# A hybrid decoder trunk: one PSUM tile for each of seven products, and 16 instead of 13 of 22 FFN double units by seven products

## The chip, the cores and the metric

The kernel runs on one core of one Trainium2 chip. Its time is the device time in microseconds of one execution; three runs are shown, and one more was taken with the hardware profiler.

## What is computed

The trunk has two layers of width 1024 over 512 tokens. The first layer mixes with stick-breaking and sparse attention heads, the second with forgetting attention; both layers end with the FFN that this change touches, and a final RMSNorm closes the kernel.

```python
def conv_glu_ffn(h, w_in, conv_w, conv_b, w_out):
    a, b = jnp.split(h @ w_in, 2, axis=-1)
    taps = conv_w[:, None, :]
    a = lax.conv_general_dilated(a, taps, window_strides=(1,), padding=[(CONV_WIDTH - 1, 0)], ...) + conv_b
    return (jax.nn.silu(a) * b) @ w_out

for layer in range(DEPTH):
    x = x + mixer(rmsnorm(x, attn_norm[layer]))
    x = x + conv_glu_ffn(rmsnorm(x, ffn_norm[layer]), ...)
return rmsnorm(x, final_norm)
```

D_FF is 2816, so each of `a` and `b` has 22 column blocks of 128.

## The kernel before, in words

Everything is kept transposed: features on the 128 partitions, the 512 tokens along the free dimension. Each fp32 operand of a matmul is split into a high and a low part (ScalarE casts the high part, VectorE subtracts it to get the low part), and each product of a block is three matmuls: high by high, low by high, high by low.

`ffn` (line 1073) runs once per layer. Its input projection is worked off in 22 **double units** (column block c of `a` and of `b`), its output projection in eight rows of `out` steps (`out`, line 1318) for each of four parts of the double units (`PARTS`, line 1070: units 0 to 5, 6 to 11, 12 to 16, 17 to 21). There are two kinds of double unit:

- `plain` (line 1157): two units of 8 contraction blocks, 24 matmuls of 512 columns each, into a PSUM tile `mm`; VectorE scales each result with `rstd` into `a` and `b`. The first `PLAIN` (line 1071) double units are of this kind.
- `seven` (line 1218): the four half-by-half blocks of tokens and contraction, for `a` and `b`, are formed from seven products of sums instead of eight products. Each product is 12 matmuls of 256 columns. The token sums (tiles `b1`, `b2`, `t1`, `t3`) are made once per FFN by `sums` (line 1191), on VectorE and GpSimd, during the plain units. The weight sums are made for every double unit: three on VectorE and one on GpSimd (`total`, line 1232, tile `sr`), each followed by a high and low split into one of eight slots (`part`, line 1241, tiles `sxh` and `sxl`). The slots are the buffers of the plain units' input, which the last plain unit frees step by step. The products (`product`, line 1265) come in the order a1, p2, p1, p4, p3, a2, b2, numbered 0 to 6. Product 3 uses part p4, whose sum needs the sums p1 and p2 first.

The readers of the seven products are one copy on ScalarE (product 0) and six additions or subtractions on VectorE, each of which also needs the one before it or two before it. After them `gate` and `gated` (lines 1104, 1121) apply the convolution, the activation and the product with `b`, and split the result into `gh` and `gl`, of which ten exist of each.

PSUM has eight banks, each 512 fp32 values wide: `mm` has two, `s` two tiles of two banks each, `t` and `o` one each. Before, products 0 and 1 shared one `s` tile, a bank for each; products 2 and 3 shared the next one; product 4 went to `o`, 5 to `t`, and 6 to a third `s` tile.

A planner (`Plan`, line 99) decides the order of all instructions of an FFN ahead of time. It takes each job's cost, the buffers it takes and gives, and a priority; on each engine the job of the best priority among those that can start goes next, and the order it finds is the program order of every engine. On TensorE a double unit (priority 100 + c) goes ahead of any out step (200 + part). All weight loads hang on SyncE's queue in one chain in program order (`M.prev_load`, lines 1229, 1230 and 1332): each waits until the one before it was issued, and for a free buffer. A second rule follows the tiles: a reader of a tile waits for the writers of that tile which stand before it in program order, and a writer for its earlier readers. Out steps of a part need the gated results of its double units, in their order.

The program order of the loads is set by the loops at the end of `ffn`:

```python
            for c in range(PLAIN):
                plain(c, root)
            ...
            done = PLAIN
            for p in range(1, len(PARTS)):
                c0, c1 = PARTS[p - 1]
                sevens(range(done, c1))
                done = max(done, c1)
                for m in range(NK):
                    if m % 2 == 0 and done < min(PARTS[p][1], c1 + 4):
                        seven(done)
                        done += 1
                    out(m, p - 1)
            sevens(range(done, NF))
```

With `PLAIN` = 9 that is: plain 0 to 8; seven 9; the eight out rows of part 0; sevens 10, 11, 12; two out rows of part 1; seven 13; two out rows; and so on to seven 21 and the out rows of part 3.

Below, a product 0 that starts at 440.54 us belongs to unit 10 of the first FFN, at 451.12 to unit 11, at 466.35 to unit 12. All instructions of the FFN are recorded by one helper, so the profile names line 83 for all of them; the tiles tell them apart.

Of the kernel before, what the change touches and what calls it, by code (L numbers as in the profile page):

```python
# [9 lines left out]
F32 = mybir.dt.float32  # L10
# [7 lines left out]
P = 128  # L18
SEQ = 512
# [15 lines left out]
class Fill:  # L35
# [5 lines left out]
    def add(self, *gens):  # L41
        self.q.extend([g, False] for g in gens)
# [115 lines left out]
def trunk(ctx, tc, A):  # L158
    nc = tc.nc
    inorder = [False]  # L160
    pe, act, dve, pool, sp = [Ordered(tc, e, inorder, e is nc.sync)
                              for e in (nc.tensor, nc.scalar, nc.vector, nc.gpsimd, nc.sync)]
# [4 lines left out]
    pp = EP(tc.tile_pool(name="pp", bufs=2, space=PSUM))  # L167

    def mm(out, l, r, st, sp_):
        pe.matmul(out, l, r, start=st, stop=sp_)  # L170

    def s_banks():
        return pp.tile([P, 2, SEQ], F32, tag="s", bufs=2, name="s")

    def s_bank():
        return s_banks()[:, 0]
# [891 lines left out]


    PARTS = ((0, 6), (6, 12), (12, 17), (17, 22))  # L1070
    PLAIN = 9

    def ffn(layer, nl, final):

# [4 lines left out]
        W = SEQ // 2  # L1079
        LO, HI = slice(0, W), slice(W, SEQ)  # L1080
        with ExitStack() as es:
# [3 lines left out]
                        a=2, tt=1, b=2, g=10, sr=2, slot=NK, sq=2)  # L1085
            plan.bufs["w"], plan.bufs["slot"] = [], []
            add = plan.add
# [6 lines left out]
            TJ = []  # L1094
# [62 lines left out]
            def plain(c, root):  # L1157
                box = {}
                ps = []
                for u in range(2):  # L1160
                    w = M.weights(A["wfi"][layer, 2 * c + u], [P, NK, P]) if c else (dict(h=first[u][0], l=first[u][1]), None)
                    lastu = (c, u) == (PLAIN - 1, 1)
                    bx, j = {}, None
# [51 lines left out]
            order = [None] * 3  # L1215
            count = [0]

            def seven(c):

                w, box, sm, sj = [None] * 4, {}, {}, {}  # L1220
                n0 = c * 0.001

                def load(u, pool_, tag):
                    def fn():
                        t = pool_.tile([P, NK, P], F32, tag=tag, bufs=2, name=tag)
                        sp.dma_start(t, A["wfi"][layer, 2 * c + u])
                        w[2 * u], w[2 * u + 1] = t[:, 0:H], t[:, H:NK]
                    return fn
                lb = add("SP", 0.35, load(1, fp, "wb"), M.prev_load, prio=1 + n0, take=("wb",), lat=3.3)
                la = M.prev_load = add("SP", 0.35, load(0, wp, "wraw"), lb, prio=1 + n0, take=("wraw",), lat=3.3)  # L1230

                def total(n, x, y, eng, *deps, give=()):
                    e = (pool, dve)[eng == "DVE"]

                    def fn():
                        sm[n] = wp.tile([P, H, P], F32, tag="sq", bufs=2, name="sr")
                        e.tensor_add(sm[n], x(), y())
                    sj[n] = order[2] = add(eng, 1.35 if eng == "POOL" else 0.69, fn, *deps, order[2], prio=1.2 + n0, take=("sr",), give=give)
                parts, pj = {}, {}

                def part(n, x, *deps, give=()):
                    def hi():
                        i = count[0] % NK
                        count[0] += 1
                        parts[n] = [xp.tile([P, H, P], F32R, tag=f"{t}{i}", name=f"s{t}") for t in ("xh", "xl")]
                        act.copy(parts[n][0], x())
                    j = order[0] = add("ACT", 0.62, hi, *deps, order[0], prio=1.2 + n0, take=("slot",))
                    pj[n] = add("DVE", 0.69, lambda: dve.tensor_sub(parts[n][1], x(), parts[n][0].bitcast(F32)), j, prio=1.2 + n0, give=give)
                E1, E3 = "DVE", "POOL"
                total("p1", lambda: w[2], lambda: w[3], E1, lb)  # L1250
                part("a1", lambda: w[0], la)
                total("p2", lambda: sm["p1"], lambda: w[0], "DVE", sj["p1"], la)
                part("p2", lambda: sm["p2"], sj["p2"])
                part("p1", lambda: sm["p1"], sj["p2"], give=("sr",))
                total("p4", lambda: sm["p2"], lambda: w[1], "DVE", pj["p2"], pj["p1"], give=("sr",))
                part("p4", lambda: sm["p4"], sj["p4"], give=("sr",))
                total("p3", lambda: w[0], lambda: w[2], E3, sj["p4"])
                part("p3", lambda: sm["p3"], sj["p3"], give=("sr",))
                part("a2", lambda: w[1], sj["p3"], give=("wraw",))
                part("b2", lambda: w[3], sj["p3"], give=("wb",))  # L1260

                s = []
                ev = []

                def product(j, n, m, take):
                    t, cols = MV[m]

                    def fn():
                        if take == "s":
                            s.append(s_banks())  # L1270
                        elif take:
                            s.append(pp.tile([P, 1, SEQ], F32, tag=take, bufs=1, name=take))
                        r = box[j] = s[-1][:, j % 2 if j < 4 else 0, 0:W]
                        h, l = parts[n]
                        for k in range(H):
                            xh, xl = B[t][0][:, k, cols], B[t][1][:, k, cols]
                            mm(r, h[:, k], xh, k == 0, False)
                            mm(r, l[:, k], xh, False, False)
                            mm(r, h[:, k], xl, False, k == H - 1)
                    order[1] = add("PE", 1.45, fn, pj[n], order[1], *TJ, prio=100 + c, take=(take,) if take else (), give=("slot",))  # L1280
                    return order[1]

                def take(eng, cost, fn, *deps, **k):
                    return add(eng, cost, fn, *deps, prio=1 + n0, **k)
                av = lambda h: box["a"][:, h]
                bv = lambda h: box["b"][:, h]

                def first_a():
                    box["a"] = fp.tile([P, SEQ], F32, tag="a", bufs=2, name="a")
                    act.copy(av(LO), box[0])  # L1290

                def first_b():
                    box["b"] = fp.tile([P, SEQ], F32, tag="b", bufs=2, name="b")
                    dve.tensor_sub(bv(LO), box[1], av(LO))

                def both():
                    b = box["b"].rearrange("p (h s) -> p h s", h=2)
                    dve.tensor_sub(b, b, box[4].unsqueeze(1).to_broadcast([P, 2, W]))
                j = product(0, "a1", "b11", "s")
                cp_ = take("ACT", 0.36, first_a, j, take=("a",))  # L1300
                j = product(1, "p2", "t2", None)
                u = take("DVE", 0.42, first_b, j, cp_, take=("b",), give=("s",))
                j = product(2, "p1", "t1", "s")
                v = take("DVE", 0.42, lambda: dve.tensor_sub(bv(HI), bv(LO), box[2]), j, u)
                j = product(3, "p4", "b22", None)
                c12 = take("DVE", 0.42, lambda: dve.tensor_sub(av(HI), box[3], bv(HI)), j, v, give=("s",))
                j = product(4, "p3", "t3", "o")
                c22 = take("DVE", 0.69, both, j, c12, give=("o",))
                j = product(5, "a2", "b21", "t")
                c11 = take("DVE", 0.42, lambda: dve.tensor_add(av(LO), av(LO), box[5]), j, u, give=("t",))  # L1310
                t = gate(c, box, c11, c12)
                j = product(6, "b2", "t4", "s")
                c21 = take("DVE", 0.42, lambda: dve.tensor_sub(bv(LO), bv(LO), box[6]), j, c22, give=("s",))
                gated(c, box, t, c21)
# [36 lines left out]
            def sevens(cs):  # L1351
                for c in cs:
                    seven(c)
            root = []
            for c in range(PLAIN):
                plain(c, root)
                if c == 0:
                    for k in range(H):
                        sums(k, root)
# [10 lines that stand above are left out]
# [265 lines left out]
```

## Time and profile before

| | |
|---|---|
| three runs | 1269.92, 1272.94, 1275.87 us; median 1272.94 |
| profiled execution | 1272.76 us, of which the span of instructions is 1271.0 us |
| granted TensorE clock, mean | 0.995 |
| busy: TensorE, VectorE, ScalarE, GpSimd | 98%, 70%, 49%, 17% of the span |
| HBM traffic | 119.28 MB read, 96 GB/s over the span |
| first FFN | about 299 to 655 us |
| second FFN | about 901 us to the end |

A row of the timeline has the start of an instruction from the start of the span, its duration, its engine, and the tile that it writes and those that it reads; in brackets stands how long the engine was idle before it and what ended that. PE is TensorE's matmuls, PEld its weight loads, DVE VectorE, ACT ScalarE, POOL GpSimd, SP SyncE. Matmuls are pipelined, so the next one starts well before the recorded end of the one before it; the pace of a stream is read from start to start.

### The profile page before, as it was taken

The page shows a single profiled execution, that of the slowest core. Times are in us where ns is not written, and L with a number is a line of the kernel's source. Part 1 is how long each engine was busy: PE and PEld are TensorE (multiplying, and loading weights), DVE is VectorE, ACT ScalarE, POOL GpSimd, SP SyncE. Part 2 cuts the span into 40 slices and gives each one's busy share as a digit, 9 for nine tenths or more (in the row PEclk, how much of TensorE's full clock was granted, in tenths as well). Part 3 has the DMA queues.
Part 4 walks back from the last instruction along what each step waited for, and adds up shares of the span by engine and source line. Part 5 has one row for each costly group of instructions (what it writes and reads, how often), then busy time and mean ns, then how long its engine had stood idle before and what let it go on. Part 6 is the DMA issues. An engine that isn't in the chain of part 4 may idle for free.

```text
span 1271.0 us, 18993 instructions
## 1 busy us (share of the span) xinstructions
PE 1243.6 (98%) x7268; PEld 1026.6 (81%) x7268; DVE 888.8 (70%) x1528; ACT 620.3 (49%) x1112; POOL 219.9 (17%) x266
## 2 busy tenths in 40 slices
PE   8999999999999999999999999999999999999997
PEld 5877776567888889999987777777788888999886
DVE  6776667548977489888863542534897759988874
ACT  5775446735543244444453654543554424444452
POOL 0000114303510000000030543300341000000011
PEclk9999999999999999999999999999999999999999
DMA  6313141112232333314233533312223233331321
GB/s 210 100 51 94 64 142 52 34 34 76 91 101 99 116 104 107 110 45 150 82 111 112 185 115 113 125 50 83 84 83 110 90 116 104 117 121 54 132 73 67
DMA packets 51418, 124.14 MB, mean 98 GB/s; under 512 B 6064, under 2 KB 17584, under 8 KB 51328
## 3 DMA queue, kind: packets, MB, share of 16 engines
q1 hardware_dynamic: 49808, 121.35, 29.7%
q10 hardware_dynamic: 1520, 1.59, 0.4%
q8 instruction: 57, 0.93, 0.3%
q14 instruction: 33, 0.27, 0.1%
HBM read 119.28 MB, written 2.13 MB: 96 GB/s over the span
## 4 chain that ended last, share of the span: by engine, by line
PE 89%; DVE 6%; ACT 3%; issue 1%; DMA 1%; SPq 0%; POOL 0%; DVEq 0%; POOLq 0%; ACTq 0%
PE mm L83 56%; PE s L83 20%; PE o L83 7%; PE t L83 7%; DVE xl L83 1%; DVE x L83 1%; DVE sxl L83 1%; DVE wlo L83 1%; ACT whi L83 0%; ACT sxh L83 0%; ACT e L83 0%; DMA x<-x 0%; DVE sr L83 0%; DVE acc L83 0%; ACT xh L83 0%
## 5 line engine op out<-in xcount | busy, mean ns | idle before, releaser
L83 PE MATMUL mm<-xh,whi 128*128 128x512 f32 x520 | 209.5, 403 | 1.6 <-ACT xh L83 1.0
L83 PE MATMUL mm<-xl,whi 128*128 128x512 f32 x520 | 203.7, 392 | 1.2 <-DVE xl L83 1.1
L83 PE MATMUL mm<-xh,wlo 128*128 128x512 f32 x520 | 203.2, 391 | 1.1 <-DVE wlo L83 1.1
L83 DVE TENSOR_TENSOR wlo<-wraw,whi 128x1024 fp32r<-128x1024 f32 (+3 forms) x95 | 114.8, 1208 | 47.0 <-ACT whi L83 46.6
L83 ACT CAST whi<-wraw 128x1024 fp32r<-128x1024 f32 (+3 forms) x95 | 96.5, 1016 | 90.3 <-PE mm L83 81.1
L83 PE MATMUL mm<-gh,wlo 128*128 128x512 f32 x332 | 129.9, 391 | 0.0
L83 PE MATMUL mm<-gh,whi 128*128 128x512 f32 x332 | 129.8, 391 | 0.0
L83 PE MATMUL mm<-gl,whi 128*128 128x512 f32 x332 | 129.2, 389 | 0.0
L83 DVE TENSOR_TENSOR x<-x,mm 128x512 f32<-128x512 f32 (+2 forms) x104 | 70.1, 675 | 77.0 <-PE mm L83 76.8
L83 PEld LDWEIGHTS mm<-xh,whi 128*128 128x128 f32 x520 | 97.7, 188 | 29.5 <-issue 7.9
L83 POOL TENSOR_TENSOR sr<-wraw,wb 128x512 f32<-128x512 f32 x26 | 36.6, 1408 | 485.2 <-DVE sr L83 359.5
L83 PEld LDWEIGHTS mm<-xl,whi 128*128 128x128 f32 x520 | 97.6, 188 | 24.5 <-DVE xl L83 3.7
L83 PEld LDWEIGHTS mm<-xh,wlo 128*128 128x128 f32 x520 | 97.8, 188 | 21.0 <-DVE wlo L83 2.1
L83 ACT CAST sxh<-sr 128x512 fp32r<-128x512 f32 x104 | 62.4, 619 | 76.9 <-DVE sr L83 59.4
L83 POOL TENSOR_SCALAR e<-e,dn 128x128 f32<-128x128 f32 (+3 forms) x128 | 70.3, 570 | 165.0 <-DVE dn L83 108.4
L83 ACT COPY ph<-t 128x512 f32<-128x512 f32 x100 | 58.5, 585 | 64.9 <-PE t L83 64.0
L83 ACT ACTIVATE e<-e,nm 128x128 f32<-128x128 f32 (+3 forms) x128 | 70.9, 557 | 31.6 <-DVE nm L83 31.6
L83 ACT ACTIVATE tt<-a,conv 128x512 f32<-128x512 f32 x44 | 36.0, 817 | 90.6 <-DVE a L83 90.3
L83 DVE TENSOR_TENSOR sxl<-sr,sxh 128x512 fp32r<-128x512 f32 x104 | 73.0, 724 | 9.3 <-ACT sxh L83 8.5
L83 DVE SCALAR_TENSOR_TENSOR tt<-a,conv,tt 128x510 f32<-128x510 f32 x88 | 72.9, 828 | 8.7 <-ACT tt L83 7.5
L83 ACT CAST whi<-wo 128x768 fp32r<-128x768 f32 (+1 forms) x60 | 47.0, 786 | 53.9 <-PE mm L83 47.9
L83 PEld LDWEIGHTS mm<-gl,whi 128*128 128x128 f32 x332 | 62.3, 188 | 13.2
(249 smaller groups left out, 3165.9 us busy)
## 6 DMA issues: line engine op xcount, KB each, us to landing
wraw<-wfi SPq DMA_DIRECT2D x62, 512.0 KB
wraw<-wu SPq DMA_DIRECT2D x31, 512.0 KB
wb<-wfi SPq DMA_DIRECT2D x26, 512.0 KB
wo<-wfo SPq DMA_DIRECT2D x32, 384.0 KB
wo<-wfo SPq DMA_DIRECT2D x28, 320.0 KB
wraw<-wo SPq DMA_DIRECT2D x16, 512.0 KB
wraw<-wv SPq DMA_DIRECT2D x10, 512.0 KB
cb<-cd SPq DMA_DIRECT2D x8, 512.0 KB
```

The source lines that it names most:

```text
L83: r = f(*a, **k)
```

## The change

The seven products each get a one-bank tile: 0, 2, 4 and 6 take `s` in turn, 1 and 5 take `t`, 3 takes `o`. The reader of each product gives its tile back. `s_bank` is the first bank of an `s` tile, so the second bank of these tiles stays unused here. `PLAIN` goes from 9 to 6, so that units 6, 7 and 8 of each FFN become sevens.

```diff
-    PLAIN = 9
+    PLAIN = 6
...
-                s = []
-                ev = []
-
                 def product(j, n, m, take):
                     t, cols = MV[m]
 
                     def fn():
                         if take == "s":
-                            s.append(s_banks())
-                        elif take:
-                            s.append(pp.tile([P, 1, SEQ], F32, tag=take, bufs=1, name=take))
-                        r = box[j] = s[-1][:, j % 2 if j < 4 else 0, 0:W]
+                            r = box[j] = s_bank()[:, 0:W]
+                        else:
+                            r = box[j] = pp.tile([P, SEQ], F32, tag=take, bufs=1, name=take)[:, 0:W]
...
-                    order[1] = add("PE", 1.45, fn, pj[n], order[1], *TJ, prio=100 + c, take=(take,) if take else (), give=("slot",))
+                    order[1] = add("PE", 1.45, fn, pj[n], order[1], *TJ, prio=100 + c, take=(take,), give=("slot",))
...
                 j = product(0, "a1", "b11", "s")
-                cp_ = take("ACT", 0.36, first_a, j, take=("a",))
-                j = product(1, "p2", "t2", None)
-                u = take("DVE", 0.42, first_b, j, cp_, take=("b",), give=("s",))
+                cp_ = take("ACT", 0.36, first_a, j, take=("a",), give=("s",))
+                j = product(1, "p2", "t2", "t")
+                u = take("DVE", 0.42, first_b, j, cp_, take=("b",), give=("t",))
                 j = product(2, "p1", "t1", "s")
-                v = take("DVE", 0.42, lambda: dve.tensor_sub(bv(HI), bv(LO), box[2]), j, u)
-                j = product(3, "p4", "b22", None)
-                c12 = take("DVE", 0.42, lambda: dve.tensor_sub(av(HI), box[3], bv(HI)), j, v, give=("s",))
-                j = product(4, "p3", "t3", "o")
-                c22 = take("DVE", 0.69, both, j, c12, give=("o",))
+                v = take("DVE", 0.42, lambda: dve.tensor_sub(bv(HI), bv(LO), box[2]), j, u, give=("s",))
+                j = product(3, "p4", "b22", "o")
+                c12 = take("DVE", 0.42, lambda: dve.tensor_sub(av(HI), box[3], bv(HI)), j, v, give=("o",))
+                j = product(4, "p3", "t3", "s")
+                c22 = take("DVE", 0.69, both, j, c12, give=("s",))
                 j = product(5, "a2", "b21", "t")
                 c11 = take("DVE", 0.42, lambda: dve.tensor_add(av(LO), av(LO), box[5]), j, u, give=("t",))
```

With `PLAIN` = 6 the loops above give: plain 0 to 5; seven 6, two out rows of part 0, seven 7, two out rows, seven 8, two out rows, seven 9, two out rows; sevens 10, 11, 12; and from there on as before.

## Rows read from the trace of the kernel before

**Rows 1.** The page, part 1: engine, busy us (share of the span), instructions

```profile
PE 1243.6 (98%) x7268; PEld 1026.6 (81%) x7268; DVE 888.8 (70%) x1528; ACT 620.3 (49%) x1112; POOL 219.9 (17%) x266
```

**Rows 2.** Three stretches, first FFN: busy us by engine, clock, DMA share, GB/s

```profile
366.00:440.00 74.00, 74.00 (x367) 62.98 (x367) 45.76 (x65) 25.59 (x37) 1.89 (x1) 1.00 0.33 108
...
440.00:492.00 52.00, 50.08 (x361) 47.27 (x360) 45.16 (x77) 24.40 (x43) 5.15 (x4) 0.97 0.27 92
...
492.00:560.00 68.00, 67.92 (x473) 63.32 (x472) 60.88 (x101) 31.47 (x54) 5.69 (x4) 1.00 0.32 100
```

**Rows 3.** Timeline of PE, second FFN: start us, us, engine, operation, out<-in

```profile
996.16 0.39 PE L83 MATMUL mm<-xh,whi 128*128 128x512 f32 x1
...
1001.60 0.28 PE L83 MATMUL s<-b1h,sxh 128*128 128x256 f32 x1
...
1090.91 0.28 PE L83 MATMUL o<-t3h,sxh 128*128 128x256 f32 x1
...
1092.35 0.28 PE L83 MATMUL t<-b2h,sxh 128*128 128x256 f32 x1
```

**Rows 4.** Timeline of PE: product 3 of units 10, 11 and their neighbours, both FFNs

```profile
444.85 0.28 PE L83 MATMUL s<-b2h,sxh 128*128 128x256 f32 x1
...
446.71 0.28 PE L83 MATMUL o<-t3h,sxh 128*128 128x256 f32 x1
...
457.13 0.38 PE L83 MATMUL s<-b2h,sxh 128*128 128x256 f32 x1 [0.15 <-ACT sxh L83]
459.13 0.58 PE L83 MATMUL s<-b2h,sxl 128*128 128x256 f32 x1 [1.61 <-DVE sxl L83]
...
459.72 0.41 PE L83 MATMUL s<-b2h,sxh 128*128 128x256 f32 x1
...
461.64 0.41 PE L83 MATMUL o<-t3h,sxh 128*128 128x256 f32 x1
...
1059.59 0.38 PE L83 MATMUL s<-b2h,sxh 128*128 128x256 f32 x1 [0.15 <-ACT sxh L83]
...
1062.99 0.28 PE L83 MATMUL o<-t3h,sxh 128*128 128x256 f32 x1
```

**Rows 5.** Timelines of PE and ACT: products 0 and 1 of units 10 and 12

```profile
443.29 0.28 PE L83 MATMUL s<-t1l,sxh 128*128 128x256 f32 x1
...
443.61 0.37 ACT L83 COPY a<-s 128x256 f32<-128x256 f32 x1 [3.12 <-PE s L83]
443.88 1.14 ACT L83 CAST sxh<-sr 128x512 fp32r<-128x512 f32 x2
...
467.67 0.28 PE L83 MATMUL s<-b1l,sxh 128*128 128x256 f32 x1
...
467.99 0.37 ACT L83 COPY a<-s 128x256 f32<-128x256 f32 x1 [1.03 <-PE s L83]
```

**Rows 6.** The tile sr, and one reader of the products: ns min/median/max

```profile
L83 DVE TENSOR_TENSOR sxl<-sr,sxh x104: 676/684/1381, 397.2 to 1219.7; 128x512 fp32r<-128x512 f32 x104
L83 DVE TENSOR_TENSOR sr<-sr,wraw x52: 679/686/693, 391.6 to 1216.1; 128x512 f32<-128x512 f32 x52
L83 POOL TENSOR_TENSOR sr<-wraw,wb x26: 1271/1296/1892, 401.6 to 1217.0; 128x512 f32<-128x512 f32 x26
...
L83 DVE TENSOR_TENSOR b<-b,s x52: 406/415/422, 403.9 to 1227.6; 128x256 f32<-128x256 f32 x52
```

**Rows 7.** Timelines of DVE and PE where the token sums end, first FFN

```profile
360.89 0.69 DVE L83 TENSOR_TENSOR t3l<-gl,t3h 128x512 fp32r<-128x512 f32 x1
...
361.06 0.39 PE L83 MATMUL mm<-xh,whi 128*128 128x512 f32 x1
```

**Rows 8.** Timeline of SP's queue, first FFN, like loads merged

```profile
385.73 42.23 SPq L83 DMA_DIRECT2D wo<-wfo  x8
```

**Rows 9.** Groups by line: busy us, mean ns, idle before; plain units on DVE

```profile
L83 DVE TENSOR_TENSOR wlo<-wraw,whi 128x1024 fp32r<-128x1024 f32 (+3 forms) x95 | 114.8, 1208 | 47.0 <-ACT whi L83 46.6
...
L83 DVE TENSOR_TENSOR a<-mm,rstd 128x512 f32<-128x512 f32 x18 | 12.4, 688 | 12.2 <-PE mm L83 12.1
```

## Prediction

> **What bounds the kernel now.** I read the page's busy table first: TensorE has work for 1243.6 of 1271.0 us [rows 1]. So only two things shorten the run: fewer matmul columns, or fewer holes in the matmul stream. Then I read the busy time by stretches of the first FFN [rows 2]: from 366 to 440 us and from 492 to 560 us TensorE is never or hardly idle (74.00 of 74, 67.92 of 68), but from 440 to 492 it lacks 1.92 us and its granted clock reads 0.97. VectorE is second: 0.62 of its time in the first of these stretches, 0.87 in the second, 0.895 in the third. Third comes the timeline of TensorE, for the pace of each kind of unit, for the places where the pace breaks, and for who is named there.
>
> **Fewer columns.** A plain double unit is two units of 24 matmuls; the last plain unit of the second FFN runs from 996.16 to 1001.60, so 5.44 us, and a double unit 10.88 us [rows 3]. A product of 12 matmuls goes from 1090.91 to 1092.35, 1.44 us; seven are 10.08 us [rows 3]. Exchanging one for the other saves 0.80 us. Three more in each of two FFNs: 6 x 0.80 = **4.8 us**, all on the path, since TensorE has no slack. The out steps, attention and the final stage are the same instructions.
>
> **The private PSUM tiles.** Products 0 and 1 lie in two banks of one tile, and so do 2 and 3. When product 1 follows product 0 at once, ScalarE's copy of product 0 should start when product 0's last matmul ends. In unit 10 it starts at 443.61, just behind the end of product 1's last matmul (443.29 + 0.28 = 443.57) [rows 5], and product 0 ended one product, 1.44 us, before that. In unit 12 an out step stands between the two, and the copy starts at 467.99, 0.04 us behind product 0's last matmul (467.67 + 0.28) while TensorE writes another tile [rows 5]. So the reader waits for the tile, 1.44 us too long, not for its bank. I count the adjacent case in six of the 13 units of each FFN. Queued behind the waiting copy on ScalarE is the cast of the fourth part (443.88 [rows 5]); behind that, VectorE's low half of this part; and product 3 waits for it.
>
> What it costs: in unit 10 product 3 takes 446.71 - 444.85 = 1.86 us in place of 1.44. In unit 11 it takes 461.64 - 457.13 = 4.51 us: VectorE's low half ends a wait at 459.13, and then matmuls come every (461.64 - 459.72) / 9 = 0.213 us in place of 0.12, the lower clock level (1.2 in place of 2.4 GHz) after that hole. The same unit of the second FFN takes 1062.99 - 1059.59 = 3.40 us, at full clock [rows 4]. Adding all smaller breaks in units whose product 1 follows at once, I get 4.84 us in the first FFN and 3.34 us in the second, 8.2 us in all; the three named here make 0.42 + 3.07 + 1.96 = 5.45 of it, and the largest others are the twin of unit 10's in the second FFN, the 0.3 us ahead of each of the two long products, and 0.3 us in unit 17 of each FFN. Units whose product 1 comes later lose only some 0.5 us together. With seven tiles the copy of 0 and the subtractions of 2 run one product earlier. Bounds on what comes back: 0 (the low half is late for want of VectorE time alone) to 8.2 us. I take **7.0**, nearer to the upper end, because the three stalls I can trace have a held copy ahead of them.
>
> The cost of the new tiles: product 1 now takes `t`, which product 5 of the unit before held; product 3 takes `o`; 4 takes `s`. At least two products (2.9 us) lie between a write and the next into the same buffer, and a subtraction takes 0.41 to 0.69 us [rows 6, 9]. I put this at nothing; the cover is those two products, and a reader later than that costs its excess.
>
> **The earlier start of the sevens.** Two orders change. First, the loads: SyncE's queue is a chain in program order. Before, the eight out-weight loads of part 0 (385.73 to 427.96 [rows 8]) stand ahead of unit 10's loads, so for 30 us TensorE does out steps only and VectorE idles, and then units 10 and 11 come with no out step left to fill their gaps. With six plain units the loads go 6, out, out, 7, out, out, 8, ..., 9, out, out, 10, 11, 12: the out steps, in front of which sevens always go, lie ready while VectorE catches up. That helps units 10 and 11 whatever the tiles do. Second, the sums of the tokens: their last VectorE step ends at 360.89 + 0.69 = 361.6, and plain unit 5's last unit, whose steps free the slots, begins at 361.06 [rows 7]. Before, 33 us lay between the sums and the first product; now none lie between the sums and the first parts, and 5.4 us to the first product (366.5). VectorE drops two weight splits of plain unit 6 (2 x 1.21 [rows 9]) and gains two sums of unit 6 (2 x 0.69 [rows 6]) there, so I do not see it later than now. Cost of this crossing: 0, to the 4 us of a start like that of units 10 and 11, per FFN. With the few tenths of a us that sevens lose elsewhere I take **1.5 us** for both FFNs.
>
> VectorE's load: a seven has 7 x 0.684 (low halves) + 3 x 0.686 (sums) [rows 6] + 5 x 0.415 + 0.69 (readers) = 9.6 us where a plain double unit has 2 x 1.21 + 2 x 0.69 = 3.8 [rows 9]: 5.8 more, 17.5 us in each FFN. From 366 to 560 it was busy 45.76 + 45.16 + 60.88 = 151.8 of 194 us [rows 2]; with 17.5 more in some 189 us that is 0.896, what the stretch from 492 to 560 already carries with 0.08 us of TensorE idle. It fits if the new order spreads it, with little to spare.
>
> One thing speaks against: GpSimd takes one of each seven's four sums (median 1.296 us), and beside it low halves last up to 1.381 in place of 0.684 us [rows 6]; six of 182 do. The Trainium skill, "SBUF — State Buffer" (Who interferes with whom), says that a VectorE instruction with two SBUF inputs and a GpSimd one that reads SBUF block each other for the whole instruction. By that rule six added sums cost VectorE up to 6 x 0.70 = 4.2 us, and if all of it reached the path the sum below would read 1266.7; the rows show such stretching from 492 to 560 with TensorE still full, so I leave it in VectorE's slack.
>
> **Sum.** Against the profiled execution, 1272.76 us (span 1271.0 and 1.8 around it; the median of the runs, 1272.94, is 0.2 above): 1272.76 - 4.8 - 7.0 + 1.5 = **1262.5 us**.
>
> **Rivals.** *Only the columns count.* Product 3 is late because its part stands at the end of a chain of VectorE sums, and stalls of the same size come back at other units. For it: the low half is named at 459.13 [rows 4], and VectorE is 0.87 busy there [rows 2]. Against: 7 of 13 units per FFN, all with their copies on time, lose next to nothing at like VectorE load. 1272.76 - 4.8 = 1268.0, no change that shows. 0.20.
> *The crossing is late.* Sums, first parts and out-weight splits meet on VectorE at 361 us, and TensorE lacks ready out steps, which want plain unit 5's gated result from the sixth step on. Against: the same crossing at 394 us was smooth. Price some 3.5 us more in each FFN: 1262.5 + 7 = 1269.5, no change. 0.08.
> *VectorE sets the pace (slower).* In units 6 to 11, where VectorE now has 9.6 us of extra work beside 10.08 us of matmuls and all gates, each unit waits for its fourth part as unit 11 did (459.13 - 457.13 - 0.12 = 1.88 us): 12 x 1.88 = 22.6, so 1272.76 - 4.8 - 8.2 + 22.6 = 1282.4. It decides from 13.0 / 12 = 1.1 us a unit, and shows as slower from 1.6. For it: the share of 0.896 and the low halves that GpSimd's sums stretch. Against: the 33 us of out steps, interleaved. 0.07.
> *The tiles do more than I count*, all small breaks go and the crossing is free: 1272.76 - 4.8 - 8.7 = 1259.3. 0.10.
>
> **The numbers.** Forecast 0.55, 1259 to 1266.5 by itself. About 0.5% (6.4 us) is what a measurement of this kernel can tell from no change, so faster is below 1266.6 and slower above 1279.3. Faster: 0.55 + 0.10 + a little of the next two = 0.67; same 0.26; slower 0.07. The range takes in the rivals at 1268.0 and 1269.5 and, below, 1259.3 with the runs' spread: 1257 to 1270.
>
> **What would show it.** After: all copies of product 0 start within 0.1 us of its last matmul; product 3 takes 1.44 us in units 10 and 11; TensorE's idle time from 440 to 492 is gone and its clock reads 1.00; out steps lie between sevens from 370 us on; the sevens of each FFN end 5 us sooner. I am wrong if product 3 still waits on VectorE's low half in several units, if TensorE idles near 366 us, or if copies still wait for the neighbour product.

## The result and the profile after

The changed kernel took 1261.28 us in the median of four runs (1261.16 to 1261.55), the kernel before 1272.87 beside it: a ratio of 0.9909, interval 0.9886 to 0.9932. The profiled execution took 1261.55 us, 11.21 less than that of before. Five more runs of the change without an edit were made later; what was expected of them names ratios of experiments shown below:

> The changed kernel once more, beside the kernel before, for the interval. If the two parts need each other (tiles alone 0.9994 to 0.9996, six plain units alone 0.9981, their product 0.998): about 0.991 again, 1260.5 to 1262 us. If the first measurement was lucky: 0.995 or more.

Measured: 1259.80 us, ratio 0.9909 (0.9893 to 0.9924).

The page of the kernel after, part 1, answers to [rows 1]:

```profile
PE 1235.4 (98%) x7484; PEld 1031.9 (82%) x7484; DVE 923.6 (73%) x1600; ACT 634.8 (50%) x1148; POOL 227.5 (18%) x272
```

TensorE is busy 8.2 us less, although it issues 216 more matmuls: two of 256 columns take the place of one of 512, and seven products that of eight. VectorE has 34.8 us more. The three stretches of [rows 2], asked of the kernel after:

```profile
366.00:440.00 74.00, 73.86 (x499) 68.22 (x498) 63.21 (x102) 32.95 (x56) 7.30 (x5) 1.00 0.27 89
440.00:492.00 52.00, 52.00 (x379) 49.36 (x378) 48.49 (x82) 25.95 (x45) 4.80 (x3) 1.00 0.31 101
492.00:560.00 68.00, 68.00 (x470) 63.57 (x469) 59.41 (x98) 31.90 (x54) 7.29 (x5) 1.00 0.27 94
```

In the middle one TensorE goes from 50.08 us to 52.00 of 52, and its clock from 0.97 to 1.00. VectorE is busy 63.21 + 48.49 + 59.41 = 171.1 of 194 us, 0.88, and spread more evenly (0.85, 0.93, 0.87) than before (0.62, 0.87, 0.895). TensorE's timeline after, products 3 and 4 of units 10 and 11 (it answers to [rows 4]):

```profile
440.82 0.28 PE L83 MATMUL o<-b2h,sxh 128*128 128x256 f32 x1
...
442.25 0.28 PE L83 MATMUL s<-t3h,sxh 128*128 128x256 f32 x1
...
453.65 0.28 PE L83 MATMUL o<-b2h,sxh 128*128 128x256 f32 x1
...
455.08 0.28 PE L83 MATMUL s<-t3h,sxh 128*128 128x256 f32 x1
```

Product 3 now takes 1.43 us in both, in place of 1.86 and 4.51. TensorE's and ScalarE's timelines after, product 0 of unit 6, the first seven:

```profile
368.17 0.28 PE L83 MATMUL s<-b1l,sxh 128*128 128x256 f32 x1
368.29 0.28 PE L83 MATMUL t<-t1h,sxh 128*128 128x256 f32 x1
...
368.49 0.37 ACT L83 COPY a<-s 128x256 f32<-128x256 f32 x1 [0.59 <-PE s L83]
```

The copy starts 0.04 us behind product 0's last matmul (368.17 + 0.28) while product 1 runs. All 32 copies of this kernel start 0.04 us behind it, whether product 1 follows at once or not.

Where the time came from, by segments: from the norm ahead of each FFN to that behind it, 354.93 became 348.59 us and 343.95 became 338.82, 6.34 + 5.13 = 11.47 us; everything outside the FFNs is 0.26 us longer. By kind: I add up, over the sevens, what each product takes above 12 x 0.12 us and each stretch of out steps above 0.227 us per matmul, and call that **the breaks** of an FFN. They were 5.39 and 3.86 us and are 1.26 and 1.32, so 6.67 us came from breaks and 11.47 - 6.67 = 4.80 from columns. What is left of them stands in three places of each FFN, all in product 3 (0.19, 0.40, 0.36 us in units 6, 7, 21). One of them, unit 7, in the timelines of VectorE and of TensorE's weight loads after:

```profile
382.84 1.81 DVE L83 TENSOR_TENSOR b<-b,tt 128x512 f32<-128x512 f32 x1
384.57 0.68 DVE L83 TENSOR_TENSOR sxl<-sr,sxh 128x512 fp32r<-128x512 f32 x1
...
385.30 0.19 PEld L83 LDWEIGHTS o<-b2h,sxl 128*128 128x128 f32 x1 [0.45 <-DVE sxl L83]
```

The product of the gate, 0.69 us elsewhere, takes 1.81 while GpSimd forms its sum (382.81 to 384.10), and the low half behind it comes too late. In units 6 and 21 the row stretched beside that sum is the low half of the gate's result (1.46 and 1.33 us).

### The profile page after: what moved, and what is told of

Same layout as the page of the kernel before. It is cut to its first block, busy times and chain, and to the rows that moved or that the text cites. A ratio compares the mean times of both kernels' runs of the same rounds, so it can differ in the third digit from the quotient of the medians.

```text
span 1259.7 us, 19517 instructions
## 1 busy us (share of the span) xinstructions
PE 1235.4 (98%) x7484; PEld 1031.9 (82%) x7484; DVE 923.6 (73%) x1600; ACT 634.8 (50%) x1148; POOL 227.5 (18%) x272
## 4 chain that ended last, share of the span: by engine, by line
PE 91%; DVE 5%; ACT 2%; issue 1%; DMA 1%; SPq 0%; POOL 0%; DVEq 0%; POOLq 0%; ACTq 0%
PE mm L83 51%; PE s L83 21%; PE t L83 11%; PE o L83 8%; DVE xl L83 1%; DVE x L83 1%; DVE wlo L83 1%; ACT whi L83 0%; DMA x<-x 0%; ACT e L83 0%; DVE sxl L83 0%; DVE acc L83 0%; ACT xh L83 0%; SPq L83 0%; DVE b L83 0%
## 5 line engine op out<-in xcount | busy, mean ns | idle before, releaser
L83 PE MATMUL mm<-xh,whi 128*128 128x512 f32 x424 | 172.2, 406 | 2.4 <-ACT xh L83 1.5
L83 PE MATMUL mm<-xl,whi 128*128 128x512 f32 x424 | 166.4, 392 | 1.1 <-DVE xl L83 1.1
L83 PE MATMUL mm<-xh,wlo 128*128 128x512 f32 x424 | 165.9, 391 | 1.1 <-DVE wlo L83 1.1
L83 DVE TENSOR_TENSOR wlo<-wraw,whi 128x1024 fp32r<-128x1024 f32 (+3 forms) x83 | 101.8, 1226 | 44.2 <-ACT whi L83 43.9
L83 ACT CAST sxh<-sr 128x512 fp32r<-128x512 f32 x128 | 76.4, 618 | 83.9 <-DVE sr L83 54.9
L83 PEld LDWEIGHTS mm<-xh,whi 128*128 128x128 f32 x424 | 79.6, 188 | 26.2 <-issue 7.9
L83 DVE TENSOR_TENSOR sxl<-sr,sxh 128x512 fp32r<-128x512 f32 x128 | 95.2, 762 | 2.7 <-ACT sxh L83 1.9
L83 PEld LDWEIGHTS mm<-xl,whi 128*128 128x128 f32 x424 | 79.6, 188 | 20.8 <-DVE xl L83 3.6
L83 PEld LDWEIGHTS mm<-xh,wlo 128*128 128x128 f32 x424 | 79.8, 188 | 17.5 <-DVE wlo L83 2.5
L83 PEld LDWEIGHTS mm<-gl,whi 128*128 128x128 f32 x332 | 62.4, 188 | 13.3
L83 PE MATMUL s<-t3l,sxh 128*128 128x256 f32 x256 | 72.4, 283 | 0.0
```

The costliest lines, as they stand in the source:

```text
L83: r = f(*a, **k)
```

## The experiments

Of the changed kernel two things had to be told apart: the tiles, and the order of units, loads and out steps that the number of plain units brings along. All ratios are to the kernel before, timed beside each run.

**The tiles alone, in the order of before.** The kernel before, each product into the bank that it has after; the planner's order is the same, row for row.

```diff
-                        if take == "s":
-                            s.append(s_banks())
-                        elif take:
-                            s.append(pp.tile([P, 1, SEQ], F32, tag=take, bufs=1, name=take))
-                        r = box[j] = s[-1][:, j % 2 if j < 4 else 0, 0:W]
+                        own = "stsosts"[j]
+                        if own == "s":
+                            r = box[j] = s_bank()[:, 0:W]
+                        else:
+                            r = box[j] = pp.tile([P, SEQ], F32, tag=own, bufs=1, name=own)[:, 0:W]
```

> The kernel before with its planner's order kept to the last instruction, nine plain units, and only the tiles of the products private. Theory A (the readers wait for a tile that the neighbour product still writes, and hold their queues): every copy of product 0 starts some 0.04 us after product 0's last matmul, product 3 of units 10 and 11 takes about 1.44 us again, and most of the 8.2 us of breaks goes: 1265.5 to 1267.5 us. Theory B (units 10 and 11 starve because no out steps are left beside them and VectorE is short of time): the breaks stay, 1271 us or more.

Measured: 1271.35 us, ratio 0.9994 (0.9983 to 1.0005). The small breaks are gone, unit 10's with them, but unit 11 still breaks. The medians hide a small gain: no run of this kernel reads a mean granted clock above 0.996, seven of the 29 runs of before beside it read 0.998. Among the runs at 0.996 the medians are 1270.1 and 1271.7 us, so some 1.6 us are saved, and the lower clock takes them back. The timelines of TensorE and GpSimd of this kernel, and below them that of VectorE:

```profile
454.54 0.28 PE L83 MATMUL o<-b2h,sxh 128*128 128x256 f32 x1
456.68 0.39 PE L83 MATMUL o<-b2h,sxl 128*128 128x256 f32 x1 [1.86 <-DVE sxl L83]
...
440.46 1.30 POOL L83 TENSOR_TENSOR sr<-wraw,wb 128x512 f32<-128x512 f32 x1 [38.79 <-DVE sr L83]
453.83 1.29 POOL L83 TENSOR_TENSOR sr<-wraw,wb 128x512 f32<-128x512 f32 x1 [12.07 <-DVE sr L83]
467.11 1.30 POOL L83 TENSOR_TENSOR sr<-wraw,wb 128x512 f32<-128x512 f32 x1 [11.99 <-ACT gh L83]
```

```profile
442.56 0.68 DVE L83 TENSOR_TENSOR sr<-wb 128x512 f32<-128x512 f32 x1
...
447.36 0.68 DVE L83 TENSOR_TENSOR sr<-sr,wraw 128x512 f32<-128x512 f32 x1
...
452.93 0.68 DVE L83 TENSOR_TENSOR sr<-sr,wraw 128x512 f32<-128x512 f32 x1
...
455.95 1.28 DVE L83 TENSOR_TENSOR sxl<-sr,sxh 128x512 fp32r<-128x512 f32 x2
```

The copy of product 0 is on time here, and product 3 still waits 1.86 us. GpSimd's sum, one per unit, shows the pace of the parts: 13.4 and 13.3 us apart. The VectorE rows are the chain of unit 11: sum p1 at 442.56, p2 at 447.36, p4 at 452.93, its low half ends at 456.63, 14 us from first to last, of which VectorE is busy 12.4. The products alone last 10.08 us. I read from this that a unit needs about 13.3 - 10.1 = 3.2 us of out steps beside it, or a lead; unit 10 of this kernel has none and unit 11 two, 1.36 us. The queue shows why none are ready (SyncE, this kernel):

```profile
383.95 42.23 SPq L83 DMA_DIRECT2D wo<-wfo  x8
426.23 0.44 SPq L83 DMA_DIRECT2D wb<-wfi  x1
427.03 0.33 SPq L83 DMA_DIRECT2D wraw<-wfi  x1
427.42 0.42 SPq L83 DMA_DIRECT2D wb<-wfi  x1
427.89 0.42 SPq L83 DMA_DIRECT2D wraw<-wfi  x1
```

Eight out loads go first, TensorE does 43 out steps in one stretch, and only then come the loads of units 10 and 11, together. In the changed kernel the same queue reads:

```profile
402.50 6.46 SPq L83 DMA_DIRECT2D wo<-wfo  x2
409.05 0.38 SPq L83 DMA_DIRECT2D wb<-wfi  x1
409.48 0.42 SPq L83 DMA_DIRECT2D wraw<-wfi  x1
412.11 4.45 SPq L83 DMA_DIRECT2D wo<-wfo  x2
416.68 0.36 SPq L83 DMA_DIRECT2D wb<-wfi  x1
```

**The change with nine plain units**, so that the planner knows of the seven tiles.

```diff
-    PLAIN = 6
+    PLAIN = 9
```

> The change's tiles and its planner tokens, with nine plain units as before. Theory A: as the run with the order of before, or up to 1 us better since the planner's order fits better: 1264.5 to 1267.5 us. Theory B: 1271 us or more.

Measured: 1271.26 us, ratio 0.9996 (0.9985 to 1.0008). Unit 11 breaks by 3.09 us in the first FFN and 2.12 in the second. The planner's order comes out as before here too, so this is nearly the same kernel as the last one. In either form, the tiles alone are worth nothing that the medians show.

**Six plain units, shared tiles.**

```diff
-    PLAIN = 9
+    PLAIN = 6
```

> Six plain units with the shared tiles of before. Both theories: 4.8 us for the columns. Theory A: the copies still wait 1.44 us wherever product 1 follows product 0 at once, so about half of the breaks come back elsewhere: 1264.5 to 1268 us. Theory B: the interleaved out steps alone fill the gaps: 1261.5 to 1263 us.

Measured: 1270.20 us, ratio 0.9981 (0.9971 to 0.9991), 2.4 us by the ratio (0.0019 x 1272), where the columns alone give 4.8: slower than both theories had it. The breaks are 5.76 and 5.80 us. The large one at unit 11 is gone, but 13 of the 16 units now have one, of 0.15 up to 1.0 us, most of them ahead of or in product 3. By tile and operation, the instructions of each engine come in the same order in the traces of this kernel, of the change and of the two kernels further down that share one pair of products. So what differs between these four is the waiting and not the order. The stretch of [rows 2] from 366 us, where TensorE was full before and is full after, in this kernel:

```profile
366.00:440.00 74.00, 72.60 (x489) 66.52 (x488) 61.49 (x100) 31.78 (x54) 6.62 (x5) 1.00 0.26 89
```

So neither half does it: by the ratios 0.5 to 0.8 us and 2.4 us alone, 11.6 together.

**Nine plain units, private tiles, another order.** Units 10 and 11 are moved between the out rows of part 0.

```diff
-    PLAIN = 6
+    PLAIN = 9
...
-                    if m % 2 == 0 and done < min(PARTS[p][1], c1 + 4):
+                    if m % 2 == 0 and done < min(PARTS[p][1], c1 + (6 if p == 1 else 4)):
```

> Nine plain units and private tiles; units 10 and 11 are put between the out rows of part 0 in the chain of loads. Theory B (what is left at unit 11 with private tiles is the burst of loads behind eight out rows and the lack of out steps beside it): the breaks of 2 to 3 us at unit 11 go in both FFNs and the clock stays at its upper level: 1263.5 to 1266 us. Theory C (unit 11 is late for VectorE's time whatever is put beside it): 1269 us or more.

Measured: 1265.55 us, ratio 0.9950 (0.9935 to 0.9965); breaks 1.50 and 1.55 us: theory B held. The order gives back what the tiles alone could not, and 1265.55 - 4.8 = 1260.8 is the change's time.

**The same order with shared tiles**: the second line of that edit, on the kernel before.

> The same order of loads with the shared tiles of before and nine plain units. Theory A with B (the order fills the gaps, the shared tiles hold queues wherever the plan runs tight): half of it, 1266 to 1270 us. If the order alone did it: as the run with private tiles, within 1 us.

Measured: 1288.77 us, ratio 1.0126 (1.0109 to 1.0143): slower, the other way from what I expected. Its breaks, with the out steps behind the sevens, are 11.3 and 12.6 us, at out steps as well as at products. One of them on TensorE:

```profile
480.34 0.50 PE L83 MATMUL mm<-gh,wlo 128*128 128x512 f32 x1 [2.04 <-DVE wlo L83]
```

The planner, too, knows the tiles that the jobs take and give, and orders VectorE's work by them; here a low half of an out weight comes too late. Which part of the loss (0.0126 x 1272 = 16 us) is the chip's waiting and which the other order isn't separated, for the order differs from that of the run above.

**Which pair of products?** Six plain units; first with products 0 and 1 apart and 2 and 3 in one tile, then the other way round. Against the kernel before:

```diff
-    PLAIN = 9
+    PLAIN = 6
...
-                        r = box[j] = s[-1][:, j % 2 if j < 4 else 0, 0:W]
+                        r = box[j] = s[-1][:, 1 if j == 3 else 0, 0:W]
...
-                j = product(1, "p2", "t2", None)
-                u = take("DVE", 0.42, first_b, j, cp_, take=("b",), give=("s",))
+                j = product(1, "p2", "t2", "t")
+                u = take("DVE", 0.42, first_b, j, cp_, take=("b",), give=("t",))
```

> Six plain units; only products 0 and 1 get tiles of their own, 2 and 3 still share one. If ScalarE's held copy of product 0 is what costs: nearly all of the change, 1261 to 1263 us. If VectorE's held readers of product 2 count as much: 1264 to 1267 us.

Measured: 1267.83 us, ratio 0.9965 (0.9955 to 0.9976), breaks 4.73 and 4.80, a little above the second forecast. TensorE and VectorE ahead of product 3 of unit 7:

```profile
383.46 0.28 PE L83 MATMUL s<-t1l,sxh 128*128 128x256 f32 x1
...
384.05 0.39 PE L83 MATMUL mm<-gl,whi 128*128 128x512 f32 x1
385.11 0.36 PE L83 MATMUL s<-b2h,sxh 128*128 128x256 f32 x1 [0.67 <-DVE b L83]
...
382.22 1.81 DVE L83 TENSOR_TENSOR b<-b,tt 128x512 f32<-128x512 f32 x1
383.95 0.68 DVE L83 TENSOR_TENSOR sxl<-sr,sxh 128x512 fp32r<-128x512 f32 x1
384.55 0.41 DVE L83 TENSOR_TENSOR b<-b,s 128x256 f32<-128x256 f32 x1
```

Here TensorE itself is held: an out step stands between products 2 and 3, so VectorE's read of product 2 (384.55) stands ahead of product 3 in program order, and product 3, a writer of the same tile, waits until it has ended, though it goes to the other bank. Its part was ready: the wait's releaser is `b`, not `sxl`. The kernel before has places that fit the same wait, units 13 and 19 of each FFN, though the profile names the cast there. In unit 13 the weight load of product 3 starts 0.11 us behind the end of VectorE's read of product 2 (487.89 + 0.41), as it does here (385.07 behind 384.55 + 0.41), and some 0.15 us are lost:

```profile
487.89 0.41 DVE L83 TENSOR_TENSOR b<-b,s 128x256 f32<-128x256 f32 x1
...
488.41 0.19 PEld L83 LDWEIGHTS s<-b2h,sxh 128*128 128x128 f32 x1 [0.36 <-ACT sxh L83]
```

Now the change, with products 0 and 1 in one tile again:

```diff
                         if take == "s":
-                            r = box[j] = s_bank()[:, 0:W]
+                            st = box["st"] = s_banks()
+                            r = box[j] = st[:, 0, 0:W]
+                        elif take is None:
+                            r = box[j] = box["st"][:, 1, 0:W]
...
-                cp_ = take("ACT", 0.36, first_a, j, take=("a",), give=("s",))
-                j = product(1, "p2", "t2", "t")
-                u = take("DVE", 0.42, first_b, j, cp_, take=("b",), give=("t",))
+                cp_ = take("ACT", 0.36, first_a, j, take=("a",))
+                j = product(1, "p2", "t2", None)
+                u = take("DVE", 0.42, first_b, j, cp_, take=("b",), give=("s",))
```

> The change, with products 0 and 1 in one tile of two banks again; products 2 and 3 and the rest keep their own. Both pairs shared with six plain units gave 1270.2 us, pair 2 and 3 shared alone 1267.8, neither 1259.8 to 1261.3. Theory A: pair 2 and 3 is what costs, because it holds TensorE itself before product 3; the held copy of product 0 has slack behind it. Then 1261 to 1263 us, copies of product 0 in units 7 and 10 again 1.48 us late, breaks per first FFN under 2 us. Theory B: the two pairs cost alike, and in e9 and e2 they only overlap: 1265 to 1268 us, breaks of some 3 us per FFN, named VectorE's low half (sxl), not b.

Measured: 1260.82 us, ratio 0.9908 (0.9892 to 0.9924): the change's own time. Unit 7 on TensorE and ScalarE:

```profile
379.61 0.28 PE L83 MATMUL s<-b1l,sxh 128*128 128x256 f32 x1
...
381.05 0.28 PE L83 MATMUL s<-t1l,sxh 128*128 128x256 f32 x1
...
381.37 0.37 ACT L83 COPY a<-s 128x256 f32<-128x256 f32 x1 [2.45 <-PE s L83]
```

The copy waits 1.48 us for the other bank, as ten of the 32 do in this kernel, and it costs nothing that can be measured: the breaks are 1.79 and 1.84 us, 0.5 per FFN above the change's. That holds with products 2 and 3 apart. With these in one tile, freeing the copy is worth about 2 us (1270.20 to 1267.83 us, ratios 0.9981 and 0.9965, breaks 1.0 us less in each FFN). The kernel before has held copies without a loss, too: of the six units per FFN whose product 1 follows at once, 9 and 16 lose nothing. In unit 9 the copy is 1.48 us late (product 0's last matmul ends at 400.73), and product 3 takes 1.43 us:

```profile
402.21 0.37 ACT L83 COPY a<-s 128x256 f32<-128x256 f32 x1 [2.04 <-PE s L83]
...
405.52 0.28 PE L83 MATMUL s<-b2h,sxh 128*128 128x256 f32 x1
...
406.95 0.28 PE L83 MATMUL o<-t3h,sxh 128*128 128x256 f32 x1
```

**Other numbers of plain units.** The change with seven, then with five.

```diff
-    PLAIN = 6
+    PLAIN = 7
```

> The change with seven plain units in place of six. Theory A: with private tiles and the interleaved order, a double unit costs just its columns: 2 x 0.80 = 1.6 us more than the change, so 1261.4 to 1263.0 us, breaks as in the change (about 1.3 us per FFN). Rival B: the time hangs on how sevens and out rows happen to stand, so another number of plain units gives breaks of several us: above 1264 us.

Measured: 1267.93 us, ratio 0.9968 (0.9957 to 0.9979); the rival held. With seven plain units the sevens 7, 8 and 9 stand between the out rows, and then 10 and 11 follow behind a stretch of 35 out steps, unit 10 again without one beside it. TensorE in unit 11:

```profile
458.79 0.39 PE L83 MATMUL o<-b2h,sxl 128*128 128x256 f32 x1 [1.86 <-DVE sxl L83]
```

It is the wait of the first experiment, to the hundredth. So a unit more or less isn't worth 0.80 us whatever the number; it depends on where the sevens fall between the out rows.

```diff
-    PLAIN = 6
+    PLAIN = 5
```

> The changed kernel with one plain unit less, five. If the token sums bind the crossing (their last VectorE step ends at 361.6 us in the kernel before; the last plain unit would end at about 355.7), the first product waits, only five out steps (3.4 us) can be put in front of it, and each FFN loses 3 to 6 us against the 0.8 us that it saves: 1265 to 1272 us. If VectorE has room at the crossing: 1259.7 us.

Measured: 1285.92 us, ratio 1.0110 (1.0097 to 1.0123), far above both forecasts. The crossing that was smooth with six plain units is not with five. TensorE and VectorE:

```profile
364.19 0.79 PE L83 MATMUL mm<-gh,whi 128*128 128x512 f32 x1 [8.32 <-ACT whi L83]
...
368.69 0.68 DVE L83 TENSOR_TENSOR t3l<-gl,t3h 128x512 fp32r<-128x512 f32 x1
```

The last token sum ends at 369.4 instead of 361.6 [rows 7], behind the first parts, which go ahead of it in VectorE's order; product 0 begins at 372.54. TensorE idles 8.32 us, until ScalarE has cast the first out weight, which stands behind the casts of the first parts. Behind the hole its matmuls of 512 columns come 0.43 us apart in place of 0.23, at the lower clock (granted 0.55 from 364 to 373 us). The last run put the sums first:

```diff
-    PLAIN = 6
+    PLAIN = 5
...
-                p = 2 + 0.1 * k
+                p = 1.1 + 0.01 * k
```

> The change with five plain units, and the token sums ahead of the sevens' parts in VectorE's order (their priority 1.1 in place of 2). Theory A: five plain units cost 26 us only because the first parts overtook the token sums, so that TensorE idled 8.3 us at the crossing and ran at its lower level behind it. With the sums first the crossing is smooth again: TensorE idles under 1 us from 340 to 380 us, the clock reads 0.99 or more, and the time is the change less the columns of two units, 1259.8 - 1.6 = 1258 us, 1256 to 1262 with breaks. Rival B: VectorE has not the time for sums and first parts in four plain units' span, whichever goes first; the first products wait for parts in place of sums: 1266 to 1286 us.

Measured: 1292.53 us, ratio 1.0164 (1.0145 to 1.0182). Theory A failed, and the rival with it: the time is above its range, and no first product waits for parts. The hole moved to a plain unit's weights, whose low half the sums now overtake.

```profile
330.74 0.79 PE L83 MATMUL mm<-xh,wlo 128*128 128x512 f32 x1 [14.99 <-DVE wlo L83]
```

With five plain units and the order of the change, VectorE is busy 60.5 of the 64 us from 300 to 364 us and still comes late, so it seems to lack the time for sums and first parts. That isn't shown: with the sums first, it is busy only 31.3 of the 41 us from 331 to 372 us, behind the hole, and no order between the two was run. Six is the fewest of those tried at which the crossing is smooth.

**GpSimd's sum on VectorE**, in the change:

```diff
-                E1, E3 = "DVE", "POOL"
+                E1, E3 = "DVE", "DVE"
```

> The change with the sum of part p3 on VectorE instead of GpSimd. VectorE gets 0.69 us more of its own in each seven, GpSimd takes no sum of the FFN. Theory A: beside GpSimd's sums VectorE's additions with two SBUF inputs are stretched by about as much as the sum would cost it (1.81 in place of 0.69 us), so VectorE's busy time from 366 to 560 us goes up by less than 16 x 0.69 = 11 us, no low half and no b is over 0.8 us, and the time stays within 2 us of the change (1259 to 1263). Rival B: the stretching is small against 0.69 us per unit; VectorE passes 0.93 busy from 366 to 560 us, product 3 and 4 wait for it, and the time is 1266 us or more.

Measured: 1267.87 us, ratio 0.9954 (0.9938 to 0.9970). Of VectorE's time the first theory was right. The windows of this kernel:

```profile
366.00:440.00 74.00, 74.00 (x505) 68.79 (x504) 65.59 (x111) 35.51 (x60) 0.00 (x0) 1.00 0.27 90
440.00:492.00 52.00, 52.00 (x376) 49.28 (x376) 47.15 (x82) 24.38 (x42) 0.00 (x0) 1.00 0.31 99
492.00:560.00 68.00, 68.00 (x460) 62.99 (x459) 59.58 (x101) 31.34 (x54) 0.00 (x0) 1.00 0.29 96
```

VectorE is busy 172.3 us in place of 171.1, though it does 12 more sums of 0.684 us here, 8.2 us: most of it comes back because nothing is stretched any more. Of the time the first theory was wrong, and the rival's figure was met for another reason: TensorE is full through these stretches, and loses at the end of the sevens, where the planner's new order leaves fewer out steps to cover the last gate (41 in place of 46 behind the last product of the first FFN). Both FFNs:

```profile
627.13 0.50 PE L83 MATMUL mm<-gh,whi 128*128 128x512 f32 x1 [1.58 <-ACT gh L83]
...
1226.61 0.50 PE L83 MATMUL mm<-gh,whi 128*128 128x512 f32 x1 [2.08 <-ACT gh L83]
```

## Why the prediction was right, and where it was not

The total was: 1262.5 forecast, 1261.28 measured, faster as forecast. Of its terms one held, one rested on the wrong cause, and one gave the new order no gain. That they still add up is luck.

- *Columns, 4.8 us*: held. 11.47 - 6.67 = 4.80, and nine plain units in the interleaved order cost 1265.55 against 1259.80 to 1261.28. It holds only at numbers of plain units that leave the order good; seven and five do not.
- *Private tiles, 7.0 us*: **this step failed**, in its cause. It charged the stalls of units 10 and 11 to the held copy of product 0. With the copies free and the order kept, unit 10's break of 0.4 us and smaller ones go, but unit 11 still breaks by over 2 us; with ten copies held and the order changed, the time is the change's. Units 9 and 16 of the trace of before, with held copies and no loss, already showed that a held copy isn't enough for a stall. The two went together in the trace of before because they have, as I read it, one cause: product 1 follows product 0 at once, and so holds the copy, where no out step is ready at that moment; and where few come ahead of product 3 either, the parts, 13.3 us a unit, fall behind the products, 10.1 us. I had the lower bound for it ("the low half is late for want of VectorE time alone") and went to the upper end because of that coincidence. What the tiles do is keep products 2 and 3 apart: in the new order, shared, they cost 1267.83 - 1260.82 = 7.0 us. That this is the figure I had put down for another reason is luck. The trace of before names no such wait in the sevens and has two places of some 0.15 us in each FFN that fit it, so this worth couldn't be read there; the order of before mostly leaves the reader of product 2 time enough.
- *The earlier start, +1.5 us*: the crossing cost 1.2 us, the breaks of units 6 and 7 (0.59 + 0.60), both behind a row of VectorE that GpSimd's sum stretched; the sentence that the interleaved rows help units 10 and 11 "whatever the tiles do" named the gain that the tiles alone don't bring, and I gave it no number. With shared tiles it is wrong as a saving: the large break goes, as many small ones come. The net of 7.0 less 1.5, 5.5, stands against 6.67 measured.
- *VectorE's load*: 0.896 forecast, 0.88 measured. *VectorE sets the pace* did not come about at this share; but its mechanism, the fourth part late in each unit that has too little beside it, is what broke unit 11 before. With five plain units it may be the bound; that isn't shown.
- *GpSimd beside VectorE*: the rows of after show the product of the gate at 1.81 in place of 0.69 us, and the sum moved to VectorE cost that engine 1.2 us in place of 8.2. The Trainium skill, "SBUF — State Buffer" (Who interferes with whom), says that a VectorE instruction with two SBUF inputs contends with a GpSimd one that reads SBUF, for a port pair that only one of them holds at a time. The trace agrees: the stretch, 1.81 - 0.69 = 1.12 us, is most of the sum's 1.29. That VectorE's slack takes it, as I had put it, held but for the 0.95 us of small breaks in each FFN, which the run with the sum on VectorE doesn't have.
- *New tiles at nothing*: held; no wait in the sevens after is for a PSUM tile.

## What to carry to other kernels

Before a stall is charged to a wait that stands ahead of it, look for what makes the two come together: here both came where filler was short, and undoing the wait alone left the median where it was. A place with the wait and without the stall (here units 9 and 16) shows before any run that the wait isn't enough. Compare the period of the chain that feeds an engine (here 13.3 us, read off the one GpSimd instruction in each unit) with what the engine does in that unit alone (10.1 us); the difference must be filled by other work, and the order of loads decides whether that work is there. Put outputs with different readers in tiles of their own, above all where a later writer would wait for the reader of the neighbour: that holds the bounding engine itself, while a reader that starts late may cost nothing (here, with products 2 and 3 apart).

## What was not expected of the hardware

Holes of about the same length leave TensorE at its full clock or not. In the change with seven plain units, unit 11's 2.1 us leave it at full clock in the first FFN, and are followed by products at the lower level in the second (1.03 us longer for the next product). In the profiled execution of before it is the other way round [rows 4]. The runs of before lie between 1269.64 and 1276.56 us, those of the change, which has no such hole, between 1259.14 and 1262.19; that the holes make the difference fits, but what decides how TensorE comes out of one isn't shown.
